# Stick-breaking attention: the two heads of a pair, interleaved or one behind the other

## The chip, the cores and the metric

The kernel runs on one core of a Trainium2 chip. The metric is the device time of one execution in microseconds (us), median of several runs. The engines named below are PE (TensorE, matrix products and transposes), ACT (ScalarE, activations and casts), DVE (VectorE, elementwise work and scans), POOL (GpSimd) and SP (SyncE, which here only issues transfers). Each engine works through its own queue in order.

## The reference, cut to what matters

One layer of a decoder trunk for 512 tokens, model width 1024, in fp32. The part that the change touches is the attention with 8 heads of width 64:

```python
z = jnp.einsum('bhqd,bhkd->bhqk', qb, kf) * scale
causal = key_pos[None, :] < q_pos[:, None]
log_beta = jax.nn.log_sigmoid(z)
log_keep = jnp.where(causal, log_beta - z, 0.0)
between = lax.cumsum(log_keep, axis=3, reverse=True) - log_keep
w = jnp.where(causal, jnp.exp(log_beta + between), 0.0)
out = jnp.einsum('bhqk,bhkd->bhqd', w, vf)
```

With beta = sigmoid(z) and keep = sigmoid(-z), the weight of a key is beta there times the product of keep over all later keys up to the query. Around it stand a projection of the normed input to q, k, v, to three convolution operands and to two gates, a short convolution with its output product, the mixing with w_o, an MLP of width 4096 and a gated embedding term.

## The kernel before, in words

All large products are done as three fp32r matmuls of a high and a low half ("split": ACT casts the high half, DVE subtracts for the low half; lines 63 to 66, so one line number stands for many places). The attention takes the heads in four pairs, `for j in range(4)`. Of one pair the order of the work on PE and SP is the order of the program (`tc.manual_schedule(engines={PE, SP})`); on ACT, DVE and POOL a planner orders the instructions beforehand, by their place in the program and by its own estimate of when each is ready, and the engine then runs that fixed queue.

On PE a pair is: `scores` (24 short matmuls, line 338), `conv_u` and `conv_b` (24 matmuls of 128x512 each), `wtrans(wa)` (the 10 transposes of the first head's weights, line 366), `proj_q` of the next pair (24 matmuls), `wtrans(wb)` (the 10 transposes of the second head's), `proj_k` of the next pair (24), then `av` twice (line 380) and `conv_c` (24). For the last pair the two projections are gates.

`scores` makes, for a tile of 128 queries at a time, the causal part of z: four blocks of 512, 384, 128 and 256 columns, 1280 columns in all, packed in three groups. Each group takes a PSUM bank for each head, so six of the eight banks. ACT reads each bank twice (line 342 gives `beta`, line 343 gives `keep`): 12 activations a pair. POOL masks the diagonal 128x128 square of each block in both (line 348): 16 a pair. DVE then runs for each head a scan over the 1280 columns from the right (line 351, in place on `keep`; `ends` starts the product anew at each block's end) and the product (line 352, in place on `beta`). The product is what `wtrans` turns.

In `conv_u` DVE reads the bank with line 397 and goes on with lines 400 and 402; in `conv_b` it reads the bank with line 407. The transposes' banks are emptied by a split into `wth` and `wtl`. `make_sums` (lines 295 to 309) prepares sums of the weights w_down for later: two loads, four subtractions (line 308) on POOL or DVE, two stores; those at low priority fall into the attention stage too.

Of the kernel before, what the change touches and what calls it, by code (L numbers as in the profile page):

```python
# [11 lines left out]
AF = mybir.ActivationFunctionType  # L12
ALU = mybir.AluOpType
# [3 lines left out]
P = 128  # L17
# [11 lines left out]
BLK = {3: (0, 512), 2: (512, 384), 0: (896, 128), 1: (1024, 256)}  # L29
# [4 lines left out]
def hybrid_block(ctx, tc, x, p, g_pre_mix, w_in, b_gate, w_conv, w_attn_out, w_conv_out, w_o,  # L34
                 g_post_mix, g_pre_mlp, w_up, w_down, g_post_mlp, g_ple, w_ple_gate, w_ple_proj, out):
    nc = tc.nc
# [17 lines left out]
    def bigt(shape, dt=F32R, name="big"):  # L54
        return big.tile(shape, dt, tag="big", name=name)

    def bank():
        return psp.tile([P, 512], F32, tag="ps", name="ps")
# [103 lines left out]
    def split_v(i):  # L162
        return split(vw[0][i // 4][:, i % 4], vw[1][i // 4][:, i % 4], vr[i // 4][:, i % 4])
# [70 lines left out]
    last = split_v(0)  # L234
# [10 lines left out]
    for k in range(2, NK):  # L245
        last = split_v(k)
# [21 lines left out]
    for t in range(2, NT):  # L268
        ps = bank()
# [23 lines left out]
    made = iter(range(NJ))  # L293
# [31 lines left out]
    def scores(st):  # L325

        beta = [bigt([P, 1280], F32, "beta") for _ in range(2)]
        keep = [bigt([P, 1280], F32, "keep") for _ in range(2)]
        for group in ((3,), (2, 0), (1,)):
            ps = [bank(), bank()]  # L330
            base = BLK[group[0]][0]
            for qb in group:
                c0, n = BLK[qb]
                c0 -= base
                for i, (a, b) in enumerate(((0, 2), (0, 3), (1, 2))):
                    for h in range(2):
                        r = slice(64 * h, 64 * h + 64)
                        nc.tensor.matmul(ps[h][:, c0:c0 + n], st[r, a, qb * P:(qb + 1) * P], st[r, b, 0:n],
                                         start=i == 0, stop=i == 2)
            n = sum(BLK[qb][1] for qb in group)  # L340
            for h in range(2):
                nc.scalar.activation(beta[h][:, base:base + n], ps[h][:, 0:n], AF.Sigmoid, scale=0.125)
                nc.scalar.activation(keep[h][:, base:base + n], ps[h][:, 0:n], AF.Sigmoid, scale=-0.125)
        for h in range(2):
            for c0, n in BLK.values():
                dg = slice(c0 + n - P, c0 + n)
                for t_, fill in ((beta[h], 0.0), (keep[h], 1.0)):
                    nc.gpsimd.affine_select(t_[:, dg], t_[:, dg], pattern=[[-1, P]], compare_op=ALU.is_gt,  # L348
                                            fill=fill, base=0, channel_multiplier=1)
            kr = keep[h][:, ::-1]  # L350
            nc.vector.tensor_tensor_scan(kr, kr, ends[:, ::-1], 1.0, op0=ALU.mult, op1=ALU.max)  # L351
            nc.vector.tensor_tensor(beta[h][:, 0:1279], beta[h][:, 0:1279], keep[h][:, 1:1280], op=ALU.mult)  # L352
        return beta

    def wtrans(w):
# [68 lines left out]
    for j in range(4):  # L424
        wa, wb = scores(st)
        y = conv_u(j, ct)
        conv_b(j, y)
        ta = wtrans(wa)
        if j < 3:
            st = proj_q(j + 1)  # L430
        else:
            sg[0] = gate(0, 0)
        tb = wtrans(wb)
        if j < 3:
            proj_k(j + 1, st)
        else:
            sg[1] = gate(0, 1)
        of = tm()
        if j in (1, 2):
            with tc.high_priority(-LATE):  # L440
                make_sums(nc.vector)
        av(2 * j, ta, of)
        av(2 * j + 1, tb, of)
        if j < 3:
            ct = conv_c(j + 1)
# [14 lines left out]
    for j in range(NK):  # L460
# [28 lines left out]
        if j == 7:  # L489
            for kk in range(2):  # L490
                ps = bank()
# [88 lines left out]
    for t in range(NT):  # L580
        tok = slice(t * P, (t + 1) * P)
        for h_ in range(2):
            cs = slice(h_ * 512, (h_ + 1) * 512)
            ps = bank()
# [289 lines left out]
    for t in range(2, NT):  # L874
        for cs in CUTS[t]:
            ps = bank()[:, 0:cs.stop - cs.start]
# [31 lines left out]
```

## Time and profile before

| | us |
|---|---|
| median of 3 runs | 741.31 (741.18 to 742.03) |
| the profiled execution | 740.8 |
| its span, first to last instruction | 739.1 |
| PE busy | 726.8 |
| DVE busy | 518.9 |
| ACT busy | 382.0 |
| POOL busy | 82.3 |

The attention pairs lie between about 53 us and 192 us of the span. A timeline row gives start, duration, engine, line, operation, output and input with their sizes, the count where equal rows were merged, and in brackets the idle time just before it with what ended that time. Where rows are merged the duration goes from the first one's start to the last one's end.

### The profile page before, as it was taken

How to read it: one execution, taken by the hardware profiler on the slowest of the kernel's cores; microseconds unless marked ns; L12 is line 12 of the kernel's file. 1: busy time of each engine (PE TensorE's matmuls, PEld its weight loads, DVE VectorE, ACT ScalarE, POOL GpSimd, SP SyncE). 2: the span in 40 equal slices, each digit the busy share in tenths (PEclk: the TensorE clock that was granted, in tenths of full speed). 3: DMA queues.
4: the chain of work that ended last, by engine and by line, in shares of the span. 5: the costliest groups of instructions: out<-in, count | busy, mean ns of one | idle time of the engine just before them, and what ended most of it. 6: DMA issues, size and time to landing. Idle time of an engine off the chain costs nothing.

```text
span 739.1 us, 10383 instructions
## 1 busy us (share of the span) xinstructions
PE 726.8 (98%) x3976; PEld 628.8 (85%) x3976; DVE 518.9 (70%) x676; ACT 382.0 (52%) x631; POOL 82.3 (11%) x124
## 2 busy tenths in 40 slices
PE   8998999999999999999999999999999999999997
PEld 7887878787888888888899999999988888888886
DVE  6767777868555524744879898977699878269762
ACT  6363545354334321432855686757776476257431
POOL 1104030312234222000200000000000000001100
PEclk9999999999999999999999999999999999999999
DMA  8591708071899876872334644432555766577311
GB/s 313 171 305 39 227 30 228 29 231 56 267 343 296 262 254 202 314 225 58 142 144 139 197 121 114 130 100 87 170 163 169 220 253 218 188 244 263 134 57 58
DMA packets 112105, 132.29 MB, mean 179 GB/s; under 512 B 4116, under 2 KB 82744, under 8 KB 111032
## 3 DMA queue, kind: packets, MB, share of 16 engines
q1 hardware_dynamic: 111464, 127.43, 54.6%
q10 hardware_dynamic: 592, 4.20, 1.4%
q8 instruction: 31, 0.51, 0.3%
q14 instruction: 18, 0.15, 0.1%
HBM read 108.55 MB, written 23.07 MB: 178 GB/s over the span
## 4 chain that ended last, share of the span: by engine, by line
PE 85%; DVE 5%; POOL 4%; DMA 3%; ACT 1%; issue 1%; SPq 1%; POOLq 0%; DVEq 0%; ACTq 0%
PE ps L90 27%; PE ps L91 27%; PE ps L92 27%; POOL keep L348 2%; DMA raw<-in_w_in_dram 2%; DVE keep L351 2%; PE ps L380 1%; PE ps L366 1%; POOL beta L348 1%; DVE beta L352 1%; PE ps L181 1%; DVE vl L65 1%; DMA wsum<-w 1%; PE ps L564 1%; DVE wlo L65 1%
## 5 line engine op out<-in xcount | busy, mean ns | idle before, releaser
L65 DVE TENSOR_TENSOR wlo<-raw,whi 128x512 fp32r<-128x512 f32 x120 | 84.8, 739 | 58.3 <-ACT whi L64 20.3
L90 PE MATMUL ps<-h1h,whi 128*128 128x512 f32 x288 | 113.6, 394 | 0.0
L92 PE MATMUL ps<-h1h,wlo 128*128 128x512 f32 x288 | 112.2, 390 | 0.0
L91 PE MATMUL ps<-h1l,whi 128*128 128x512 f32 x288 | 112.2, 389 | 0.0
L64 ACT CAST whi<-raw 128x512 fp32r<-128x512 f32 x120 | 69.0, 623 | 47.7 <-DMA raw<-in_w_in_dram 20.4
L90 PE MATMUL ps<-w,sb 128*128 128x512 f32 x216 | 84.1, 389 | 0.0
L92 PE MATMUL ps<-w,sb 128*128 128x512 f32 x216 | 84.0, 389 | 0.0
L91 PE MATMUL ps<-w,sb 128*128 128x512 f32 x216 | 84.0, 389 | 0.0
L65 DVE TENSOR_TENSOR w<-raw,w 128x1024 fp32r<-128x1024 f32 x56 | 67.4, 1219 | 20.7 <-PE ps L91 11.3
L64 ACT CAST w<-raw 128x1024 fp32r<-128x1024 f32 x56 | 58.4, 1052 | 36.4 <-DMA raw<-wsum 17.9
L92 PEld LDWEIGHTS ps<-h1h,wlo 128*128 128x128 f32 x288 | 54.1, 188 | 11.4
L90 PEld LDWEIGHTS ps<-h1h,whi 128*128 128x128 f32 x288 | 54.1, 188 | 11.3
L90 PE MATMUL ps<-h2h,us 128*128 128x256 f32 x224 | 63.5, 283 | 0.0
L91 PE MATMUL ps<-h2l,us 128*128 128x256 f32 x224 | 63.4, 283 | 0.0
L92 PE MATMUL ps<-h2h,us 128*128 128x256 f32 x224 | 63.4, 283 | 0.0
L91 PEld LDWEIGHTS ps<-h1l,whi 128*128 128x128 f32 x288 | 54.1, 188 | 10.7
L132 POOL TENSOR_TENSOR rs<-ms,mhalf 128x1 f32<-128x1 f32 x20 | 14.9, 745 | 417.8 <-DVE ms L128 364.8
L65 DVE TENSOR_TENSOR us<-raw,us 128x1024 fp32r<-128x1024 f32 x42 | 50.6, 1218 | 6.1 <-ACT us L64 6.0
L64 ACT CAST us<-raw 128x1024 fp32r<-128x1024 f32 x42 | 43.3, 1050 | 16.6 <-DVE raw L663 7.7
L90 PEld LDWEIGHTS ps<-w,sb 128*128 128x128 f32 x216 | 40.5, 188 | 8.5
L90 PE MATMUL ps<-tb,us 128*128 128x256 f32 x168 | 47.7, 284 | 0.0
L91 PEld LDWEIGHTS ps<-w,sb 128*128 128x128 f32 x216 | 40.5, 188 | 8.4
(206 smaller groups left out, 1638.7 us busy)
## 6 DMA issues: line engine op xcount, KB each, us to landing
raw<-in_w_in_dram SPq DMA_DIRECT2D x36, 512.0 KB, 6.3
w<-in_w_down_dram SPq DMA_DIRECT2D x32, 512.0 KB, 4.9
wsum<-w SPq DMA_DIRECT2D x32, 512.0 KB, 3.6
raw<-in_w_up_dram SPq DMA_DIRECT2D x32, 512.0 KB, 4.4
raw<-wsum SPq DMA_DIRECT2D x32, 512.0 KB, 5.4
raw<-in_w_down_dram SPq DMA_DIRECT2D x24, 512.0 KB, 4.1
raw<-in_w_o_dram SPq DMA_DIRECT2D x8, 512.0 KB, 5.9
raw<-in_w_ple_gate_dram SPq DMA_DIRECT2D x8, 512.0 KB, 7.5
```

Of the source, the lines that this page charges most:

```text
L64: a = nc.scalar.copy(hi, src)
L65: b = nc.vector.tensor_tensor(lo, src, hi.bitcast(F32), op=ALU.subtract)
L90: nc.tensor.matmul(ps, lh, rh, start=start, stop=False, skip_group_check=onto)
L91: nc.tensor.matmul(ps, lh, rl, start=False, stop=False, skip_group_check=onto)
L92: nc.tensor.matmul(ps, ll, rh, start=False, stop=stop, skip_group_check=onto)
L132: nc.gpsimd.tensor_tensor(r, m, mhalf, op=ALU.pow)
L181: nc.tensor.transpose(warm[:, 0:P], ident, ident)
L348: nc.gpsimd.affine_select(t_[:, dg], t_[:, dg], pattern=[[-1, P]], compare_op=ALU.is_gt, fill=fill, base=0, channel_multiplier=1)
L351: nc.vector.tensor_tensor_scan(kr, kr, ends[:, ::-1], 1.0, op0=ALU.mult, op1=ALU.max)
L352: nc.vector.tensor_tensor(beta[h][:, 0:1279], beta[h][:, 0:1279], keep[h][:, 1:1280], op=ALU.mult)
L366: nc.tensor.transpose(ps[:, c0 + (qb - kb) * P:c0 + (qb - kb + 1) * P], w[:, o:o + P], ident)
L380: nc.tensor.matmul(ps[:, kb * P:S], lhs, wt[i][:, c0:c0 + n], start=(kb == 0 and i == 0), stop=(kb == NT - 1 and i == 1))
```

## The change

`scores` no longer runs its activations in the loop over the groups. It keeps the list of groups with their banks, and a helper `chain(h)` emits for one head: the three `keep` activations, the three `beta` activations, the four masks of `keep`, the four masks of `beta`, the scan and the product. It returns the last `beta` activation and the product. The second head's chain is emitted inside `tc.issue_after` of both: its ACT instructions are placed behind the first head's last activation in ACT's queue, its DVE instructions behind the first head's product in DVE's queue. POOL gets no such order. The matmuls, the number of instructions and their sizes stay.

```diff
+        made = []
...
-            n = sum(BLK[qb][1] for qb in group)
-            for h in range(2):
-                nc.scalar.activation(beta[h][:, base:base + n], ps[h][:, 0:n], AF.Sigmoid, scale=0.125)
-                nc.scalar.activation(keep[h][:, base:base + n], ps[h][:, 0:n], AF.Sigmoid, scale=-0.125)
-        for h in range(2):
-            for c0, n in BLK.values():
-                dg = slice(c0 + n - P, c0 + n)
-                for t_, fill in ((beta[h], 0.0), (keep[h], 1.0)):
+            made.append((base, sum(BLK[qb][1] for qb in group), ps))
+
+        def chain(h):
+            for t_, sign in ((keep[h], -1), (beta[h], 1)):
+                for base, n, ps in made:
+                    last = nc.scalar.activation(t_[:, base:base + n], ps[h][:, 0:n], AF.Sigmoid, scale=0.125 * sign)
+            for t_, fill in ((keep[h], 1.0), (beta[h], 0.0)):
+                for c0, n in BLK.values():
+                    dg = slice(c0 + n - P, c0 + n)
                     nc.gpsimd.affine_select(t_[:, dg], t_[:, dg], pattern=[[-1, P]], compare_op=ALU.is_gt,
                                             fill=fill, base=0, channel_multiplier=1)
             kr = keep[h][:, ::-1]
             nc.vector.tensor_tensor_scan(kr, kr, ends[:, ::-1], 1.0, op0=ALU.mult, op1=ALU.max)
-            nc.vector.tensor_tensor(beta[h][:, 0:1279], beta[h][:, 0:1279], keep[h][:, 1:1280], op=ALU.mult)
+            done = nc.vector.tensor_tensor(beta[h][:, 0:1279], beta[h][:, 0:1279], keep[h][:, 1:1280], op=ALU.mult)
+            return last, done
+
+        last, done = chain(0)
+        with tc.issue_after(last.ins), tc.issue_after(done.ins):
+            chain(1)
         return beta
```

## The prediction

> **What bounds the kernel now.** I began with the page's busy times and PE's waits, then PE's timeline to place each wait, then the queues of DVE, POOL and ACT in front of it.
>
> ```profile
> PE 726.8 (98%) x3976; PEld 628.8 (85%) x3976; DVE 518.9 (70%) x676; ACT 382.0 (52%) x631; POOL 82.3 (11%) x124
> PE ps L366 <- DVE beta L352: 5.9, 4, 2.1
> PE ps L181 <- POOL ident masks.py:199: 1.4, 1, 1.4
> 68.45 1.28 PE L366 MATMUL ps<-ident,beta 128*128 128x128 f32 x10 [2.15 <-DVE beta L352]
> 104.37 1.28 PE L366 MATMUL ps<-ident,beta 128*128 128x128 f32 x10 [1.37 <-DVE beta L352]
> 140.62 1.28 PE L366 MATMUL ps<-ident,beta 128*128 128x128 f32 x10 [1.68 <-DVE beta L352]
> 175.84 1.28 PE L366 MATMUL ps<-ident,beta 128*128 128x128 f32 x10 [0.67 <-DVE beta L352]
> ```
>
> PE bounds the program: it is busy for 726.8 of 739.1 us. Of its waits, only one group lies inside the program: four times, once in each pair, the transposes of the first head's weights wait for that head's product: 2.15 + 1.37 + 1.68 + 0.67 = 5.87 us. That is the most that this change can return through PE. No PE instruction changes, and the rest of PE's idle time is at the start and the end.
>
> The first pair shows why the product is late.
>
> ```profile
> 54.63 0.60 ACT L342 ACTIVATE beta<-ps 128x512 f32<-128x512 f32 x1
> 55.12 0.60 ACT L343 ACTIVATE keep<-ps 128x512 f32<-128x512 f32 x1
> 57.36 0.62 ACT L64 CAST whi<-raw 128x512 fp32r<-128x512 f32 x1 [0.66 <-DMA wsum<-w]
> 60.07 0.42 ACT L343 ACTIVATE keep<-ps 128x256 f32<-128x256 f32 x1
> 60.86 1.72 ACT L64 CAST whi<-raw 128x512 fp32r<-128x512 f32 x3
> 56.97 0.74 POOL L348 TENSOR_SCALAR_AFFINE_SELECT keep<-keep 128x128 f32<-128x128 f32 x1
> 60.75 0.30 POOL L348 TENSOR_SCALAR_AFFINE_SELECT keep<-keep 128x128 f32<-128x128 f32 x1
> 61.00 0.30 POOL L348 TENSOR_SCALAR_AFFINE_SELECT beta<-beta 128x128 f32<-128x128 f32 x1
> 61.24 2.82 POOL L348 TENSOR_SCALAR_AFFINE_SELECT keep<-keep 128x128 f32<-128x128 f32 x1
> 56.17 1.39 DVE L65 TENSOR_TENSOR wlo<-raw,whi 128x512 fp32r<-128x512 f32 x2 [1.94 <-DMA wsum<-w]
> 61.09 5.83 DVE L351 TENSOR_TENSOR_SCAN keep<-keep,ends 128x1280 f32<-128x1280 f32 x2 [3.53 <-POOL keep L348]
> 66.84 2.87 DVE L352 TENSOR_TENSOR beta<-beta,keep 128x1279 f32<-128x1279 f32 x2
> 69.62 0.68 DVE L397 TENSOR_TENSOR tmp<-tmp,ps 128x512 f32<-128x512 f32 x1
> ```
>
> Two delays sit ahead of the first product. The first head's last keep activation (60.07) is the tenth of twelve, so the first scan starts only at 61.09. Then DVE runs both scans before either product: the first head's product begins at 66.84, a whole scan (5.83 / 2 = 2.92) later than its own scan allows. It ends near 68.31 (half of the 2.87, rounded up for overlap) and PE starts at 68.45.
>
> **The change part by part.** Nothing is added or removed: 12 activations, 16 masks, two scans and two products a pair, all at their old sizes; no transfer moves and SP's queue is untouched. Four things move.
>
> *Keep first on ACT.* The first head's last keep activation becomes the third. At a pitch of 0.49 (54.63 to 55.12) it starts 0.98 after the first; the scan follows it by 1.02 as now (60.07 to 61.09), so 2.0 after the first activation. The other pairs:
>
> ```profile
> 91.33 0.60 ACT L342 ACTIVATE beta<-ps 128x512 f32<-128x512 f32 x1
> 97.01 5.83 DVE L351 TENSOR_TENSOR_SCAN keep<-keep,ends 128x1280 f32<-128x1280 f32 x2 [4.67 <-POOL keep L348]
> 127.27 0.60 ACT L342 ACTIVATE beta<-ps 128x512 f32<-128x512 f32 x1
> 128.40 1.39 DVE L65 TENSOR_TENSOR wlo<-raw,whi 128x512 fp32r<-128x512 f32 x2 [1.58 <-ACT keep L343]
> 133.26 5.84 DVE L351 TENSOR_TENSOR_SCAN keep<-keep,ends 128x1280 f32<-128x1280 f32 x2 [3.48 <-POOL keep L348]
> 162.93 0.60 ACT L342 ACTIVATE beta<-ps 128x512 f32<-128x512 f32 x1 [0.37 <-PE ps L338]
> 165.38 0.69 DVE L308 TENSOR_TENSOR w<-w,w 128x512 f32<-128x512 f32 x1 [2.60 <-DMA w<-in_w_down_dram]
> 168.48 5.83 DVE L351 TENSOR_TENSOR_SCAN keep<-keep,ends 128x1280 f32<-128x1280 f32 x2 [2.40 <-POOL keep L348]
> ```
>
> That gives 56.6, 93.3, 129.3 and 164.9. But I leave the DVE work that now precedes the scan in front of it, since it ends later in three pairs: 57.56, 129.79, 166.07. With 0.2 for the last mask behind it: 57.8, 93.3, 130.0, 166.1. So the first scan starts 3.3, 3.7, 3.3 and 2.4 us earlier. Call this d. Its lower bound is zero (the planner undoes it), the upper 4.5 in the first pair (61.09 − 56.6).
>
> *Masks behind the scan.* This is a new cost. The mask issued at 61.24, as the scan began, took 2.82 instead of 0.30 and ended with the scan; one issued during the 0.6 us split at 56.97 took 0.74. So POOL stands still under such DVE work. After the change all four beta masks of a head are due while its scan runs. As at 61.00, one gets through; the other three resume at the scan's end, the first finishing there and two more at 0.25 each: 0.5, with 0.1 to release the product. If POOL were not held the cost would be 0; if head two's masks were queued in front, 1.0 more. I take 0.6, the row's own pattern. The second head's keep masks meet the first product in the same way; no row shows a mask beside this product, so it costs between 0 and 0.6; I take 0.6 from the split's row.
>
> *Product straight after its scan.* First product's end: scan start + 2.9 + 0.6 + 1.5 = +5.0, where now it is +7.2 (61.09 to 68.31). Earlier by d + 2.2: 5.5, 5.9, 5.5, 4.6 us, against stalls of 2.15, 1.37, 1.68 and 0.67. All four go, with 3 us to spare; even at d = 0 the 2.2 covers the longest one. The cover of what I cost at nothing here is `conv_u` and `conv_b` on PE, 11 us behind the scores.
>
> *The second head waits.* Its product ends at scan start + 5.0 + 0.6 + 2.9 + 0.6 + 1.4 = +10.5, where now both are done at +8.53 (61.09 to 69.62). Against today it ends 1.97 − d later, that is 1.3, 1.7, 1.3 and 0.4 earlier. Behind it on DVE stand the convolution's operations, of which L407 frees `conv_b`'s bank, and later the first head's wtl. Who needs that bank is `proj_k` on PE, which follows the second head's transposes:
>
> ```profile
> 74.34 0.68 DVE L407 TENSOR_TENSOR tmp<-ps,tmp 128x512 f32<-128x512 f32 x1
> 76.06 0.48 PE L90 MATMUL ps<-h1h,whi 128*128 128x512 f32 x1
> 110.38 0.68 DVE L407 TENSOR_TENSOR tmp<-ps,tmp 128x512 f32<-128x512 f32 x1
> 111.14 1.09 PE ps L366 x10
> 146.64 0.68 DVE L407 TENSOR_TENSOR tmp<-ps,tmp 128x512 f32<-128x512 f32 x1
> 147.39 1.09 PE ps L366 x10
> 181.86 0.68 DVE L407 TENSOR_TENSOR tmp<-ps,tmp 128x512 f32<-128x512 f32 x1
> 182.62 1.09 PE ps L366 x10
> ```
>
> At that point three banks of each transposed head, `proj_q`'s and `conv_b`'s make eight of eight. The slack now is 76.06 − 75.02 = 1.04, then 112.23 − 111.06 = 1.17, 1.16 and 1.17. PE will come earlier by its old stall, L407 by d − 1.97: slack 0.2, 1.5, 0.8, 0.9. Thin in the first pair, but no new wait. The score banks of the second head stay full some 2 us longer in ACT's queue; the next user is the transposes, about 10 us later. Weights are far ahead: the split at 56.17 belongs to the next pair's `conv_u`, some 35 us later.
>
> The sum is made against the profiled execution: 740.8 − 5.87 = 734.9 (span 739.1, the other 1.7 lie around it). The median stands 0.5 above it, so 735.4.
>
> **The rivals.**
>
> *A: POOL's stalls eat the lead.* If the planner keeps the keep activations late or puts DVE work into the new gaps, d shrinks; the second head then holds L407 back. New wait in a pair = old stall + (1.97 − d) − slack. At d = 2: 1.1 + 0.2 + 0.5 + 0 = 1.8, time 737.2. At d = 1: 2.1 + 1.2 + 1.5 + 0.5 = 5.3, time 740.7. At d = 0: 3.1 + 2.2 + 2.5 + 1.5 = 9.3, time 744.8. It is back at no change near d = 0.9. For it: the stretched masks above, and the cast and the splits that already stand among the activations. Against it: seven of the nine activations ahead of the first head's last keep leave, which DVE work cannot undo; and in pairs two and three the first wtl frees a bank before L407 does, so the waits are upper bounds. The Trainium skill, "SBUF — State Buffer", section "SBUF: two separate sides", speaks for this rival: a DVE operation with two SBUF inputs and a GpSimd operation take a port pair as an exclusive lock, whoever starts first holds it for its whole instruction. The trace agrees (2.82 against 0.30); by it a mask that starts first would also delay scan and product, up to 0.25 each, an estimate from the mask's pitch.
>
> *B: slower, by a cast.* ACT's queue can get a weight cast between the first head's last activation and the second's first, as it has one at 57.36 now, waiting 0.66 for a buffer. If that buffer were freed only by `conv_b` (PE ends it at 68.45 − 2.15 = 66.30), the second head starts at about 66.9 and its product ends at 66.9 + 2.0 + 2.9 + 0.6 + 1.4 = 73.8, 4.2 later than 69.62; wait in pair one 2.15 + 4.2 − 1.04 = 5.3. If all four pairs had it, about 20 us: 741.3 − 5.9 + 21 = 756. One pair is even; from two pairs on it is slower. Against it: the three casts at 60.86 run without a wait, long before `conv_b` ends.
>
> *C: the change does not do what it says.* If the scans stayed together on DVE, only d would come: the product earlier by d alone, which still covers every stall (735.4). So this does not separate by time, only by the trace; its small chance is within the forecast's.
>
> **How the numbers follow.** The forecast, all four waits gone: 0.62, 734.8 to 736.2, the width being what runs differ (741.18 to 742.03). Rival A between d = 2.4 and 1.2, 736.2 to 739.8: 0.18. A near its even point, together with one pair of B: 0.11, within 0.2% (1.5 us, about what a measurement can tell here). B in several pairs or A below d = 0.5: 0.09, slower. The range 734.8 to 739.8 holds 0.80; faster 0.80.
>
> **What would show it.** In the trace after: PE's waits have no row for L366 on L352; first scan near 58, 91, 126 and 161 (57.8, 93.3, 130.0, 166.1, less the stalls gone before each); DVE in the order scan, product, scan, product with gaps of 0.5 to 0.7 ahead of each product (ended by POOL beta); two stretched masks a head; the second product ending no later than now relative to the scores. Wrong would be: PE waits at `proj_k` for L407 or wtl (A), a cast with a long wait between the activations on ACT (B), or the waits at L366 still there.

## The result, and the profile after

The changed kernel takes 738.30 us (median of 5 runs, 738.16 to 739.35), the kernel before 742.03 (5 runs beside it, 741.18 to 743.75). The ratio of the runs is 0.9945, 95% interval 0.9933 to 0.9956, which is 4.1 us; the two medians differ by 3.7. The forecast was 5.9 us less. The profiled execution took 738.92 us with a span of 737.2, before 740.8 and 739.1.

PE's waits in the changed kernel, by cause (total, times, longest):

```profile
PE ps L90 <- DVE tmp L414: 3.8, 3, 1.7
PE ps L181 <- POOL ident masks.py:199: 1.4, 1, 1.4
```

The row of 5.9 us at the first transposes (now line 373) is gone. A new row stands in its place: three times the first matmul of `proj_k` waits for L414, the DVE product of `conv_b` (L407 before). The difference is 5.87 − 3.8 = 2.1 us, and the spans differ by 1.9. PE's timeline places the three:

```profile
75.63 0.50 PE L90 MATMUL ps<-h1h,whi 128*128 128x512 f32 x1 [1.66 <-DVE tmp L414]
110.67 0.50 PE L90 MATMUL ps<-h1h,whi 128*128 128x512 f32 x1 [0.39 <-DVE tmp L414]
147.01 0.50 PE L90 MATMUL ps<-h1h,whi 128*128 128x512 f32 x1 [1.71 <-DVE tmp L414]
```

The first pair on ACT, POOL and DVE in the changed kernel (L346 activations, L350 masks, L353 scan, L354 product):

```profile
54.64 0.60 ACT L346 ACTIVATE keep<-ps 128x512 f32<-128x512 f32 x1
55.12 0.60 ACT L346 ACTIVATE beta<-ps 128x512 f32<-128x512 f32 x1
57.75 1.14 ACT L64 CAST whi<-raw 128x512 fp32r<-128x512 f32 x2 [2.02 <-DMA wsum<-w]
58.80 0.59 ACT L346 ACTIVATE keep<-ps 128x512 f32<-128x512 f32 x1
59.76 0.38 ACT L346 ACTIVATE keep<-ps 128x256 f32<-128x256 f32 x1
60.97 4.74 POOL L350 TENSOR_SCALAR_AFFINE_SELECT keep<-keep 128x128 f32<-128x128 f32 x4
65.67 3.54 POOL L350 TENSOR_SCALAR_AFFINE_SELECT beta<-beta 128x128 f32<-128x128 f32 x4
60.76 2.89 DVE L353 TENSOR_TENSOR_SCAN keep<-keep,ends 128x1280 f32<-128x1280 f32 x1 [2.95 <-POOL keep L350]
63.75 1.57 DVE L354 TENSOR_TENSOR beta<-beta,keep 128x1279 f32<-128x1279 f32 x1
65.75 2.89 DVE L353 TENSOR_TENSOR_SCAN keep<-keep,ends 128x1280 f32<-128x1280 f32 x1 [0.43 <-POOL keep L350]
69.24 1.49 DVE L354 TENSOR_TENSOR beta<-beta,keep 128x1279 f32<-128x1279 f32 x1 [0.61 <-POOL beta L350]
70.65 0.68 DVE L404 TENSOR_TENSOR tmp<-tmp,ps 128x512 f32<-128x512 f32 x1
74.90 0.68 DVE L414 TENSOR_TENSOR tmp<-ps,tmp 128x512 f32<-128x512 f32 x1
```

DVE runs scan, product, scan, product, as meant. But ACT runs keep and beta alternately, group by group, and two weight casts stand after the first group, where ACT waits 2.02 us for a store of sums to free the buffer. So the scan starts at 60.76, only 0.33 earlier than before. The second head's masks are then held under the scans and the first product (four in 4.74 us, four in 3.54), and the second product ends near 70.7, about 1 us later than before. L414 comes behind it, at 74.90 where L407 stood at 74.34 before, while PE, no longer held up by the first transposes, comes some 2.1 earlier.

### The profile page after: what moved, and what is told of

It is laid out like the page before. It is cut to its first block, busy times and chain, and to the rows that moved or that the text cites. A ratio compares the mean times of both kernels' runs of the same rounds, so it can differ in the third digit from the quotient of the medians.

```text
span 737.2 us, 10389 instructions
## 1 busy us (share of the span) xinstructions
PE 727.1 (99%) x3976; PEld 629.2 (85%) x3976; DVE 520.6 (71%) x676; ACT 381.9 (52%) x631; POOL 96.6 (13%) x124
```

## The experiments

The theory from this profile (theory 1): the product-first order on DVE brings the gain; the late start of the scan (the cast) and the held masks make the second product late, L414 with it, and PE waits for the bank that L414 frees. In each diff only the edit is shown.

**One part alone: the edge on DVE, on the kernel before.**

```diff
-        for h in range(2):
+        def chain(h):
...
+            return done
+        done = chain(0)
+        with tc.issue_after(done.ins):
+            chain(1)
```

> The kernel before, with one edge added: the second head's DVE work is placed behind the first head's product (scan, product, scan, product). ACT and POOL keep the queue of before. Theory 1 (the first product waited for the second scan; what was gained is lost again because the second product, and with it the release of conv_b's bank, comes late): the first product is 2.9 us earlier, all four waits at the first transposes (5.87) go; the second product ends as before, since only one mask meets the first scan, so proj_k waits at most 1.1 + 0.2 + 0.5 + 0 = 1.8. PE idle in the pairs 1 to 2 us, the time 737 to 738 against 742.03 before, so at or under the changed kernel's 738.30. Rival (the new order of activations and masks is what helps): the time stays near 741.

Measured: 735.92 us (734.79 to 737.09) against 742.36 before, ratio 0.9918 (0.9901 to 0.9935). The one edge is better than the whole change: its slowest run lies below the fastest of the changed kernel (738.16). It is also better than expected (737 to 738), since `proj_k` waits 0.4 us in one pair where up to 1.8 was allowed. What is left of PE's waits in its pairs:

```profile
PE ps L90 <- DVE tmp L413: 0.4, 1, 0.4
```

**The other part alone: the changed kernel without that edge.**

```diff
-        with tc.issue_after(last.ins), tc.issue_after(done.ins):
+        with tc.issue_after(last.ins):
```

> The changed kernel without the edge on DVE: ACT and POOL have the same queues, DVE runs scan, scan, product, product. Theory 1: the second scan waits for keep masks held under the first (until about 64.4 in pair one), the first product starts near 67.3 and ends near 68.8, so the waits at the first transposes are back at 5 to 6 us in all, as before or slightly more; time 740.5 to 743. Rival (the new order of activations and masks alone helps): the waits at the transposes go with the scans side by side, time near 738.3.

Measured: 740.90 (739.84 to 742.67), ratio 0.9984 (0.9972 to 0.9996). PE's waits are back at the first transposes, and DVE's timeline shows the second scan held up by its masks. The row of waits names the masks of `beta` on POOL; but the first product ends at 68.62 and PE starts at 68.77, as close behind it as in the kernel before (68.30 and 68.45), so the rows do not tell the two apart:

```profile
PE ps L373 <- POOL beta L350: 5.5, 3, 2.5
```

```profile
60.56 2.89 DVE L353 TENSOR_TENSOR_SCAN keep<-keep,ends 128x1280 f32<-128x1280 f32 x1 [2.90 <-POOL keep L350]
64.30 2.89 DVE L353 TENSOR_TENSOR_SCAN keep<-keep,ends 128x1280 f32<-128x1280 f32 x1 [0.85 <-POOL keep L350]
67.12 1.50 DVE L354 TENSOR_TENSOR beta<-beta,keep 128x1279 f32<-128x1279 f32 x1
```

The new order of activations and masks gives little by itself, 0.2%.

**The cast moved behind the activations, in the changed kernel.**

```diff
-        ps = proj(wcols(w_in, 1536 + c * P), hx)
+        with tc.issue_after(behind[c - 1]) if c else ExitStack():
+            wb_ = wcols(w_in, 1536 + c * P)
+        ps = proj(wb_, hx)
...
+        behind[j] = acts[-1].ins
```

`acts` collects the activations of `scores`, so `behind[j]` is the last one of pair j; `wb_` holds the weights of `conv_b`.

> The changed kernel, with the cast of conv_b's weights of the next pair placed behind this pair's last activation on ACT (it stood between the first and the second group's activations and waited 2.02, 0.62 and 1.95 us there for a store of sums). Theory 1: the first scan starts 2 to 2.8 us earlier in three pairs, the second product and L414 with it, the waits of proj_k (3.8 in the profile) go; time 734 to 735.5. Rival (the bank or POOL's masks hold PE, not the start of the scan): proj_k waits as long as now, 738.3.

Measured: 734.14 (733.69 to 734.78), ratio 0.9895 (0.9880 to 0.9910). PE's waits in the pairs are gone; one of 0.6 us at a weight split lies far behind them, at 697 us. ACT and DVE in the first pair:

```profile
55.99 0.42 ACT L350 ACTIVATE keep<-ps 128x256 f32<-128x256 f32 x1
57.02 2.88 DVE L357 TENSOR_TENSOR_SCAN keep<-keep,ends 128x1280 f32<-128x1280 f32 x1 [2.72 <-POOL keep L354]
72.08 0.68 DVE L421 TENSOR_TENSOR tmp<-ps,tmp 128x512 f32<-128x512 f32 x1
```

The third keep activation comes 3.8 us earlier (55.99 for 59.76), the scan 3.7, the release of the bank 2.8 (72.08 for 74.90). That settles the place of the loss: the casts in ACT's queue. The edit moved more than it names: the planner also put two casts behind that stood just ahead of the first activation (53.60 in the changed kernel), so this activation starts at 54.07 instead of 54.64; of the 3.8 us some 0.6 are theirs.

**The second head without its masks** (this leaves the causal masks of every second head out).

```diff
-                for c0, n in BLK.values():
+                for c0, n in BLK.values() if h == 0 else ():
```

> The changed kernel without the eight masks of each pair's second head (leaves the causal masks of every second head out). Theory 1: the gaps of 0.43 and 0.61 in front of the second scan and the second product go, the second product ends 1.0 earlier, proj_k's waits of 1.66, 0.39 and 1.71 fall to about 0.6, 0 and 0.7; time 735.5 to 736.5. Rival (masks lie beside other work): no change, 738.3.

Measured: 735.37 (734.58 to 736.33), ratio 0.9910 (0.9896 to 0.9925). That is a little less than expected. The scan starts nearly as late as in the changed kernel (60.35 for 60.76), but nothing holds what follows:

```profile
60.35 2.88 DVE L353 TENSOR_TENSOR_SCAN keep<-keep,ends 128x1280 f32<-128x1280 f32 x1 [2.95 <-POOL keep L350]
64.74 2.82 DVE L353 TENSOR_TENSOR_SCAN keep<-keep,ends 128x1280 f32<-128x1280 f32 x1
67.67 1.49 DVE L354 TENSOR_TENSOR beta<-beta,keep 128x1279 f32<-128x1279 f32 x1
```

```profile
PE ps L90 <- DVE tmp L414: 0.2, 1, 0.2
```

So taking the held masks away is worth 2.9 us and taking the casts away 4.2, where all waits at `proj_k` were 3.8: either one is enough to end nearly all of them, and the two do not add up.

**The bank freed by ACT, the lateness left in.**

```diff
-        nc.vector.tensor_tensor(y, ps, y, op=ALU.mult)
+        yb = tm()
+        nc.scalar.copy(yb, ps)
+        nc.vector.tensor_tensor(y, yb, y, op=ALU.mult)
```

> The changed kernel, with conv_b's bank copied out by ACT (idle there from about 64 to 75 us in pair one) before DVE multiplies; the scans start as late as in the changed kernel. Theory 1: proj_k waited for that one bank alone, so its waits of 1.66, 0.39 and 1.71 go though the second product is as late as now; time 734.5 to 736. Rival (PE waits for the second product or the wtl splits, the bank is only what the profile names): waits of 1 to 2 us come back at the second transposes or at the first wtl, time 737.5 to 738.3.

Measured: 734.54 (733.99 to 735.20), ratio 0.9891 (0.9869 to 0.9912). PE has no wait left in the pairs, though L404 starts at 69.90 and the product that was L414 at 74.75, later than PE's first matmul of `proj_k` (73.47):

```profile
69.90 0.68 DVE L404 TENSOR_TENSOR tmp<-tmp,ps 128x512 f32<-128x512 f32 x1
74.75 0.68 DVE L416 TENSOR_TENSOR tmp<-tmp 128x512 f32<-128x512 f32 x1
```

It was the bank that PE waited for, not the arithmetic.

**The cast moved, on the kernel before; and both edges on the kernel before.** The edits are those of the first and the third experiment.

> The kernel before with only the cast of conv_b's weights of the next pair placed behind this pair's last activation; interleaved activations and masks, scan, scan, product, product stay. Theory 1 (what the start of the scan costs): without the casts and their waits the first scan starts 1 to 2 us earlier in three pairs, against waits at the first transposes of 2.15, 1.37, 1.68 and 0.67; 0.2, 0, 0 and 0.7 are left and nothing new comes, time 736 to 738 where before has 742.4. Rival (only the order of scan and product on DVE matters): 740 or more.

> The kernel before with two edges and none of the new chain: the second head's DVE work behind the first head's product, and the cast of conv_b's weights of the next pair behind this pair's last activation. Theory 1: no PE wait is left in the pairs in either this or the changed kernel with the cast behind (734.14 there), so the time is the same, 733.7 to 734.8; the new order of activations and masks is worth nothing once the scan is early. Rival (the new chain carries part of that gain): 735.5 or more.

Measured: 736.28 (736.14 to 739.40) with the cast alone, ratio 0.9922 (0.9902 to 0.9943), and 734.11 (734.04 to 734.77) with both, ratio 0.9887 (0.9866 to 0.9909), beside 742.50 for the kernel before. With the cast alone, the old order scan, scan, product, product stays, and it starts 1.9 us earlier (59.22 for 61.09), which leaves 1.4 us of waits. As in the third experiment the two casts ahead of the first activation went behind too, and 0.6 of the 1.9 are theirs:

```profile
59.22 5.83 DVE L355 TENSOR_TENSOR_SCAN keep<-keep,ends 128x1280 f32<-128x1280 f32 x2 [4.94 <-POOL keep L352]
```

```profile
PE ps L370 <- DVE beta L356: 0.8, 3, 0.3
PE ps L370 <- ACT whi L64: 0.6, 1, 0.6
```

With both there is no PE wait in the pairs. It equals the changed kernel with the cast moved (734.14): once the scan is early and the product stands straight behind it, the new order of activations and masks is worth nothing.

**Keep really first.**

```diff
-                for base, n, ps in made:
-                    last = nc.scalar.activation(t_[:, base:base + n], ps[h][:, 0:n], AF.Sigmoid, scale=0.125 * sign)
+                with tc.issue_after(last.ins) if sign > 0 else ExitStack():
+                    for base, n, ps in made:
+                        last = nc.scalar.activation(t_[:, base:base + n], ps[h][:, 0:n], AF.Sigmoid, scale=0.125 * sign)
```

> The changed kernel, with the three beta activations of a head also placed behind its three keep activations, so that ACT and POOL run keep, keep, keep, beta, beta, beta, as the forecast took the change to do; the cast stays between. Theory 1: the first scan starts 0.5 us earlier, but now three beta masks are held under it and the first product waits 0.5 to 0.6 after its scan; the second product is as late as now, time 738.3 plus or minus 0.6, proj_k's waits as now. Rival (keep first is what the change lacked): the second product 1 us or more earlier, time 736.5 or less.

Measured: 738.97 (738.35 to 741.15), ratio 0.9955 (0.9940 to 0.9970). DVE's timeline has the forecast's pattern of three gaps, each ended by masks:

```profile
60.65 2.91 DVE L354 TENSOR_TENSOR_SCAN keep<-keep,ends 128x1280 f32<-128x1280 f32 x1 [2.48 <-POOL keep L351]
64.18 1.55 DVE L355 TENSOR_TENSOR beta<-beta,keep 128x1279 f32<-128x1279 f32 x1 [0.61 <-POOL beta L351]
66.41 2.89 DVE L354 TENSOR_TENSOR_SCAN keep<-keep,ends 128x1280 f32<-128x1280 f32 x1 [0.68 <-POOL keep L351]
69.91 1.49 DVE L355 TENSOR_TENSOR beta<-beta,keep 128x1279 f32<-128x1279 f32 x1 [0.62 <-POOL beta L351]
```

In this execution ACT waited 2.98 us at the cast, so the half us of keep first was lost there, and the second product ends later still. The time is that of the changed kernel within the two intervals.

**Both kernels profiled again.**

> The kernel before, profiled once more. Its 31 timed runs beside the experiments spread from 740.2 to 744.7 with a median near 742.4, the profiled one had 740.8, and the kernels without a PE wait in the pairs spread by 0.7 to 1.2 us. Theory 1 (the spread is the landing of the sums' stores, passed on by the cast in ACT's queue to the scan and to PE): whatever this run has above 740.8 stands in the four waits at the first transposes, 5.87 plus the excess within 0.5 us, and the wait of the cast in pair one is longer than 0.66 by about that pair's share. Rival (the spread has nothing to do with the pairs): the waits are 5.9 again and the excess lies elsewhere.

> The changed kernel, profiled once more; the first profiled execution had 738.9 with 3.8 us of waits at proj_k, the runs 738.16 to 739.35. Theory 1: the waits at proj_k are 3.8 plus or minus what this run's time differs from 738.9, within 0.5 us. Rival: the waits are the same and the time differs elsewhere.

Measured: the kernel before 743.42, span 741.7, 2.6 more than in the first profile; its waits at the transposes are 6.3, only 0.4 more. One link of theory 1 holds: in pair one the cast waits 1.04 instead of 0.66, and PE 2.51 instead of 2.15. But it does not explain the 2.6 us; the rest is elsewhere. PE's timeline and the windows show where (columns: window, length, busy time of PE, PEld, DVE, ACT and POOL, then the granted clock, DMA share and GB/s):

```profile
68.82 2.32 PE L367 MATMUL ps<-ident,beta 128*128 128x128 f32 x10 [2.51 <-DVE beta L353]
```

```profile
65.48:68.89 3.41, 0.90 (x5) 0.47 (x4) 3.41 (x3) 0.00 (x0) 0.00 (x0) 1.00 0.41 143
68.89:72.30 3.41, 3.41 (x14) 3.12 (x15) 3.41 (x6) 0.00 (x0) 0.00 (x0) 0.50 0.03 11
```

The wait is 2.51 us here instead of 2.15, and after it the granted clock is 0.5 for 3.4 us. The ten transposes take 2.32 instead of 1.28. By the windows over the whole span PE is busy 2.2 us longer than in the first profile (728.95 against 726.76). So this wait of 2.5 us cost nearly twice itself. The changed kernel taken again was 739.65, 0.7 more, with waits at `proj_k` of 3.4, that is 0.4 less; the surplus is 1.2 us of waits outside the pairs, 0.4 at 3.8 us and 0.8 at 702 us. My expectation missed there too: the time of one execution and its waits in the pairs need not agree within half a us.

**A wait made on purpose, on the kernel with both edges and no waits** (`ends` times `ends` leaves it as it is; two or three times).

```diff
+            with ExitStack() as held:
+                for _ in range(3 if h == 0 else 0):
+                    fill_ = nc.vector.tensor_tensor(ends, ends, ends, op=ALU.mult)
+                    held.enter_context(tc.issue_after(fill_.ins))
...
```

> The kernel with both edges and no PE wait in the pairs (734.11), with two idle-making DVE products of 1.4 us (ends times ends, which leaves ends as it is) placed ahead of each pair's first product, so that PE waits some 1.0 to 1.6 us at the first transposes of each pair. Theory 3 (from the profile of the kernel before taken again: after a wait of 2.51 us the granted clock was 0.5 for some 3.4 us, after one of 2.15 it stayed 1.00, and that lost 1.7 us more): the waits stay under 2.2, the clock stays 1.00, the time is 734.1 plus the waits (4 to 6 us), 738 to 740.5, PE's busy time as before. Rival (a wait costs only itself at any length, the lost time came from elsewhere): the same here.

> The same with three such products, so that PE waits some 2.5 to 3.6 us at the first transposes of each pair. Theory 3: after most of the waits the granted clock falls to 0.5 for about 3.4 us and PE's busy time grows by 1.7 us each; the time is 734.1 plus the waits (11 to 14 us) plus 5 to 7 us, 750 to 755. Rival (a wait costs only itself): 745 to 748, the granted clock 1.00 throughout the pairs.

Measured: 741.83 (741.15 to 743.08) with the short waits, 756.75 (754.53 to 758.47) with the long ones, for 734.11 without. PE's waits and PE's row of the page, first with the short waits, then with the long:

```profile
PE ps L380 <- DVE beta L361: 5.7, 4, 1.6
PE ps L92 <- DVE tmp L423: 0.9, 1, 0.9
```

```profile
PE 727.1 (98%) x3976; PEld 628.7 (85%) x3976; DVE 530.7 (72%) x684; ACT 381.7 (52%) x631; POOL 81.1 (11%) x124
```

```profile
PE ps L380 <- DVE beta L361: 13.8, 4, 3.5
```

```profile
PE 735.3 (97%) x3976; PEld 635.7 (84%) x3976; DVE 537.2 (71%) x688; ACT 382.7 (51%) x631; POOL 80.5 (11%) x124
```

With waits up to 1.6 us the clock stays at 1.00, and PE is busy 1.0 us longer than in the kernel without waits (727.1 for 726.1). With four waits of 3.3 to 3.5 us PE is busy another 8.2 us longer for the same matmuls, 2.05 a wait. Both times came out above what I expected. The short ones did so by 1.3 us: the waits (6.9 in all) and the 1.0 of busy time bring the span of 732.4 to 740.3, where 740.5 was measured; why PE is busy 1.0 longer at full clock stays open. The long ones did so at least in part because I put each drop of the clock at 3.4 us: of the four, two last 3.4 us and two 6.8 (108.51 to 115.33 and 149.47 to 156.29).

## Why the prediction was right, and which terms were wrong

*What bounds the kernel* was right: in every profile without a drop of the clock inside the program PE is busy for 725.8 to 727.1 us, so the spans differ by PE's waits.

*Product straight after its scan* was right and carries the gain: all four waits at the first transposes went, and this edge alone gave 735.92.

*Keep first on ACT* was the term that failed. I took the third activation to be the first head's last keep and the scan to start 2.0 us after the first activation. Scan start less first activation, before and after: 6.46 and 6.12, 5.68 and 4.72, 5.99 and 6.04, 5.55 and 3.44, so the lead d was 0.3, 1.0, −0.05 and 2.1 instead of 3.3, 3.7, 3.3 and 2.4. The last keep of the first head became the fifth activation and not the third, since the planner kept keep and beta alternating. The rows of the changed kernel for pairs two to four:

```profile
90.95 0.60 ACT L346 ACTIVATE keep<-ps 128x512 f32<-128x512 f32 x1
95.67 2.88 DVE L353 TENSOR_TENSOR_SCAN keep<-keep,ends 128x1280 f32<-128x1280 f32 x1 [2.85 <-POOL keep L350]
125.97 0.60 ACT L346 ACTIVATE keep<-ps 128x512 f32<-128x512 f32 x1
132.01 2.89 DVE L353 TENSOR_TENSOR_SCAN keep<-keep,ends 128x1280 f32<-128x1280 f32 x1 [2.86 <-POOL keep L350]
161.75 0.60 ACT L346 ACTIVATE keep<-ps 128x512 f32<-128x512 f32 x1 [0.37 <-PE ps L339]
165.19 2.89 DVE L353 TENSOR_TENSOR_SCAN keep<-keep,ends 128x1280 f32<-128x1280 f32 x1 [0.18 <-POOL keep L350]
```

I had seen the cast at 57.36 and counted it for the second head only (rival B); it stands in front of the first head's second group, and its wait grew from 0.66 to 2.02, mostly because ACT reaches it 1 us sooner while the store lands no sooner (the cast starts at 57.36 before and 57.75 after). Only the fourth pair has no cast there, and its d is nearly the forecast's.

*Masks behind the scan*: the size was right (0.43 and 0.61 for 0.6 each; 0.61, 0.68 and 0.62 in the kernel with keep really first). The first head escaped it in the changed kernel, as its beta masks ran before the scan. POOL stands still under the product too, which no row had shown before: of the four masks that take 4.74 us, one takes 2.76 under the scan and one 1.54 under the product. This is the lock of the Trainium skill, "SBUF — State Buffer", section "SBUF: two separate sides"; the trace agrees (0.29 for a mask beside neither).

*The second head waits*: the chain from scan to second product's end is 9.9, for 10.5 forecast. Its consequence was named and placed rightly in rival A, at `proj_k` through `conv_b`'s bank. The slack in pairs two to four was read 0.25 too large: the first matmul of `proj_k` starts there at 111.98, 148.24 and 183.46, so the slack was 0.92 each time, where 1.17, 1.16 and 1.17 were taken. With it the rival's formula gives 2.7, 1.5, 2.8 and 0 for the d measured, where 1.66, 0.39, 1.71 and 0 came. Taking 9.9 for 10.5 makes it 2.1, 0.9, 2.2 and 0, and the 0.5 that is still too much in each of three pairs fits one split less on DVE between the second product and the read of the bank (three of 0.6 us in the changed kernel, four before).

*The range* held, and in part by luck. I gave A 0.18 between 736.2 and 739.8 and the full gain 0.62; 738.3 is A. But A's part of the range was drawn for d between 1.2 and 2.4, and the d measured is below that in three pairs. With these d the rival's formula, slack mended, adds 7.0 us and leaves no gain at all, 742.4; it was the shorter chain and the one split less, neither of them in the formula, that brought the time back into the range.

*The median*: I put it 0.5 above the profiled execution and took that for noise. Of 31 runs of the kernel before beside the first eight experiments, 16 show a granted clock of at most 0.998 over the span, and their median is 743.2; the other 15 have 741.7. The first profile, at 740.8, was a low one without a drop of the clock inside the program. So the 5.87 us that I called the most the change can return had left the clock out, a term put at nothing: the kernel with both edges lies 8.4 below the kernel before in the medians. That the changed kernel gains more in the medians (3.7) than in its waits (2.1) fits this, since its waits stay at 1.7 or less; it is argued from the clocks, not shown run by run.

## What to carry to other kernels

When an edge is drawn to bring a chain forward, look in the queue of its first engine for foreign work that waits for a transfer: here weight casts cost about as much as the reorder earned, and moving them alone gave 736.28 (the reorder alone 735.92). Ask for each buffer behind the chain's end who waits for it; one copy by an idle engine, 734.54, did as much as mending the order. The smallest edit that names the bottleneck (product before the second scan, one edge) beat the rearrangement that contained it.

## What the runs showed of the hardware

A wait of PE of 2 to 2.5 us may halve the granted clock for 3.4 us afterwards, and its length alone does not decide it. In the run without the product edge a wait of 2.47 us leaves the clock at 1.00 and one of 2.52 does not; in the run with keep really first one of 2.43 halves it, at 76.86; in the kernel before one of 2.15 does not. The rows are those of the run without the product edge, then one of the run with long waits (columns as above):

```profile
68.77 1.28 PE L373 MATMUL ps<-ident,beta 128*128 128x128 f32 x10 [2.47 <-POOL beta L350]
140.94 1.51 PE L373 MATMUL ps<-ident,beta 128*128 128x128 f32 x10 [2.52 <-POOL beta L350]
66.77:70.18 3.41, 1.41 (x12) 1.40 (x13) 2.98 (x3) 0.00 (x0) 2.25 (x3) 1.00 0.44 154
138.45:141.86 3.41, 0.92 (x9) 0.95 (x10) 2.98 (x3) 0.20 (x1) 2.74 (x3) 1.00 0.45 154
141.86:145.27 3.41, 3.41 (x12) 2.74 (x11) 3.38 (x6) 0.87 (x2) 0.00 (x0) 0.50 0.00 0
```

```profile
67.55:70.96 3.41, 1.33 (x11) 1.34 (x12) 3.41 (x3) 0.00 (x0) 0.00 (x0) 1.00 0.34 131
```

The Trainium skill, "TensorE: Matmul & The Clock Gate", section "What's actually happening", gives an idle window of about 3.4 us that runs free of the kernel; the length at half rate agrees, but here no window had to be idle throughout.

The traces fit windows of 3.41 us, counted back and forth from the drops that each of them shows. The wait of 2.47 falls into two such windows, 0.47 and 2.00 us, and that of 2.52 almost whole into one, 2.49. In all the profiles every window between 13 us and the last matmul in which PE idles for 2.08 us or more (2.08 in the last row above, then 2.43, 2.49, 2.51, 2.72, 2.76 and 2.80) is followed by a drop, and none with 2.00 or less is. That is seven drops, worked out afterwards; no run was made to test it. By it a wait of somewhat over 2 us halves the clock in some executions and not in others, which would make a kernel's times spread: the kernel before varies from 740.2 to 744.7, the one with both edges from 734.0 to 734.8. That this is the reason of the spread is argued, not shown.
